# Multiplying 56 gating column tiles by the first two feature tiles ahead of their turn, with new chunk sizes

## The chip, the cores and the metric

One NeuronCore of a Trainium2 chip runs the whole program in one launch. The metric is device time in microseconds, the median of a few executions. One execution was also recorded by the hardware profiler, and every time below is from that record unless it is called a median. Engines are named as in the profile: PE multiplies matrices and PEld is its weight load, DVE and ACT are the vector and the scalar engine, POOL is GpSimd, SP issues all DMAs.

## The reference

One block of a diffusion backbone on 256 latent tokens and 256 context tokens, with 4096 features (16 tokens' rows and batch are dropped here):

```python
mod = jax.nn.silu(c) @ w_ada + b_ada                    # 4096 x 12288, c is a vector
shift, scale, gate = jnp.split(mod, 3, axis=-1)
h = modulate(rmsnorm(x, g_norm), shift[:, None], scale[:, None])
proj = h @ w_in                                         # 4096 x 16384
xa, xb, ga, gb = jnp.split(proj, [LRU_W, MIX_W, MIX_W + LRU_W], axis=-1)
hc = modulate(rmsnorm(ctx, g_norm), shift_c, scale_c)   # the same w_ada, on c_ctx
xa_c = hc @ w_in[:, :LRU_W]                             # context needs xa alone
ya, ya_c = rglru_branch(xa, xa_c, conv_w, conv_b, lam, w_r, b_r, w_i, b_i, ctx_out)
yb = pool_branch(xb.reshape(Bn, rows, GRID_W, POOL_W), w_pool, b_pool, pool_scale)
mixed = jnp.concatenate([ya * jax.nn.silu(ga), yb * jax.nn.silu(gb)], axis=-1)
x_new = x + gate[:, None] * (mixed @ w_out)             # 8192 x 4096
return rmsnorm(x_new, g_final)
```

All is float32. The kernel reaches that precision by splitting both sides of a product into a high part (`hi`, rounded to the fast float32r) and the rest (`lo`), and multiplying hi by hi, hi by lo and lo by hi.

## The kernel before

Activations lie with features on the 128 partitions and tokens along the free axis, so 4096 features are 32 feature tiles `x[k]` of 128 x 512: 256 latent tokens, then 256 context tokens. Weights come from HBM in tiles of 128 x 1024 (512 KB). `load_w` puts one into a buffer of the `raw` pool (6 buffers), lets ACT round it to `hi` (4 buffers, L97) and DVE or POOL subtract to get `lo` (3 buffers, L99). The vector products with `w_ada` take raw tiles as they are.

**Start.** All 32 x tiles are loaded and squared for the token statistics (L393 to L410). After every third one (`X_STEP`) a `w_ss` tile of the first chunk is loaded and multiplied on PE (L237). A product with ones (L412) gives the sums of squares, `rstd_of` the factor `rstd`, and `prep_h` makes of an x tile the modulated activation: times `rstd` on DVE (L300; L416 for the first chunk), scale and shift on ACT (L303), the split into `hhi` on ACT (L130) and `hlo` on DVE (L131).

**xa stage.** The features are handled in chunks (`CHUNKS`: two tiles, two, then four at a time, nine chunks in all; called c0 to c8 here). In chunk c PE multiplies the chunk's activations by all 32 column tiles of the xa part of `w_in`, three matmuls of 512 columns for each pair of feature and column tile (L337 to L339). The sums of the chunks are added in SBUF: c0 copies with ACT, later ones add with POOL (L345, L346) or DVE (L348). Under these matmuls the shift and scale columns of the next chunk are made: each `w_ss` tile is multiplied into an accumulator by DVE (L213, two instructions of 1024 columns for a tile) or, for `SHARES[c]` of a chunk's tiles, on PE (L237). At the chunk's end `rows` and `cols` turn the sums into columns (L237, L192, L202 to L204), three `prep_h` follow, and a fourth stands behind the chunk. A quarter of the chunk after the next is begun early (`EARLY`, `LAGS`).

**Gating stage.** PE multiplies the kept latent activations `hT` (32 tiles, hi beside lo) by the remaining 48 blocks of 256 columns of `w_in`: 16 pooling blocks, 16 gating blocks for yb, 16 gating blocks for ya. A block takes 8 weight tiles, each with 4 feature tiles x 2 halves x (one matmul of 512 columns, L566, and one of 256, L567). The evacuation of a gating block folds the two parts (L543, L548), applies the sigmoid and multiplies. The recurrent branch runs beside it, head by head, on DVE and ACT, with its own gate products (L478 to L480).

**Output stage.** 16 blocks of `w_out` by the mixed activations, the residual and the final norm, with the rest of the `gate` columns beside it.

The code writes a list of events; `run` issues the loads `LOOK` (4) weight tiles or `LOOK_A` (2) `w_ada` tiles ahead of their use. A scheduler then sets the order of each engine's instructions and of SP's DMAs, and engines run them in that order. The pools on which this change rests: `slots` (61 tiles of 128 x 512: x, `acc`, `hT` and more), `temps` (14), `ps_mm` (4 PSUM tiles of 512 columns).

## Time and profile before

| | us |
|---|---|
| median of 3 executions (2993.66 to 2999.54) | 2995.32 |
| span of the profiled execution | 2998.8 |
| start, up to the first xa matmul | 65.8 |
| xa stage | 803.9 |
| gating stage | 1354.3 |
| output stage with the end | 774.9 |

The profiled execution has no other time than its span on its page; the span lies 3.5 us above the median and within the three executions. The stages are cut at the first matmul of the next stage. In the rows further down a stretch's row gives its length, then for PE, PEld, DVE, ACT and POOL in this order how much of it the engine was busy (with the number of its instructions), the clock that PE was granted, the mean busy share of the 16 DMA engines, and the GB/s that they moved.

### The profile page before, as it was taken

How to read it: one execution, taken by the hardware profiler on the slowest of the kernel's cores; microseconds unless marked ns; L12 is line 12 of the kernel's file. 1: busy time of each engine (PE TensorE's matmuls, PEld its weight loads, DVE VectorE, ACT ScalarE, POOL GpSimd, SP SyncE). 2: the span in 40 equal slices, each digit the busy share in tenths (PEclk: the TensorE clock that was granted, in tenths of full speed). 3: DMA queues.
4: the chain of work that ended last, by engine and by line, in shares of the span. 5: the costliest groups of instructions: out<-in, count | busy, mean ns of one | idle time of the engine just before them, and what ended most of it. 6: DMA issues, size and time to landing. Idle time of an engine off the chain costs nothing.

```text
span 2998.8 us, 40342 instructions
## 1 busy us (share of the span) xinstructions
PE 2909.6 (97%) x14992; PEld 2405.3 (80%) x14992; DVE 2256.7 (75%) x2661; ACT 1559.9 (52%) x2112; POOL 530.7 (18%) x304
## 2 busy tenths in 40 slices
PE   5999999999999999999999999999999999999997
PEld 2656777778788888888888888888888888878886
DVE  6999999998447788888777777778888766665444
ACT  4442344434436666677666666666464443333442
POOL 1466777777520000000000000000000000000000
PEclk9999999999999999999999999999999999999998
DMA  8777787887365555565665566667978888786665
GB/s 301 279 261 252 262 263 261 272 277 250 126 183 176 176 177 175 179 183 172 186 185 181 185 188 189 196 195 251 326 232 318 318 288 286 264 279 216 193 191 171
DMA packets 201142, 679.47 MB, mean 227 GB/s; under 512 B 22000, under 2 KB 30320, under 8 KB 200944
## 3 DMA queue, kind: packets, MB, share of 16 engines
q1 hardware_dynamic: 200944, 676.89, 68.9%
q8 instruction: 117, 1.92, 0.3%
q14 instruction: 81, 0.66, 0.1%
HBM read 661.60 MB, written 15.20 MB: 226 GB/s over the span
## 4 chain that ended last, share of the span: by engine, by line
PE 84%; DVE 6%; DMA 6%; issue 1%; POOL 1%; ACT 1%; SPq 0%; DVEq 0%; POOLq 0%; ACTq 0%
PE mm L566 38%; PE mm L567 19%; PE mm L337 6%; PE mm L338 6%; PE mm L339 6%; DMA raw<-in_w_gate 4%; DVE wide L213 3%; PE wide L478 2%; PE wide L480 2%; PE wide L479 2%; PE mm L237 2%; DMA raw<-in_w_ss 1%; DMA x<-in_xc 1%; DVE lo L99 1%; DVE hlo L131 1%
## 5 line engine op out<-in xcount | busy, mean ns | idle before, releaser
L97 ACT CAST hi<-raw 128x1024 fp32r<-128x1024 f32 x832 | 871.9, 1049 | 968.6 <-PE mm L566 576.3
L99 DVE TENSOR_TENSOR lo<-raw,hi 128x1024 fp32r<-128x1024 f32 x704 | 856.5, 1221 | 371.5 <-PE mm L567 282.7
L566 PE MATMUL mm<-hT,hi 128*128 128x512 f32 x3072 | 1086.8, 399 | 0.0
L567 PE MATMUL mm<-hT,lo 128*128 128x256 f32 x3072 | 862.7, 281 | 0.0
L213 DVE SCALAR_TENSOR_TENSOR wide<-raw,sc,wide 128x1024 f32<-128x1024 f32 (+1 forms) x556 | 662.4, 1240 | 153.5 <-DMA raw<-in_w_gate 119.6
L566 PE MATMUL mm<-mix,hi 128*128 128x512 f32 x2048 | 724.7, 398 | 0.0
L566 PEld LDWEIGHTS mm<-hT,hi 128*128 128x128 f32 x3072 | 577.2, 188 | 144.5 <-ACT mix L130 0.9
L567 PE MATMUL mm<-mix,lo 128*128 128x256 f32 x2048 | 577.4, 282 | 15.3 <-DVE lo L99 15.1
L567 PEld LDWEIGHTS mm<-hT,lo 128*128 128x128 f32 x3072 | 580.2, 189 | 1.3
L566 PEld LDWEIGHTS mm<-mix,hi 128*128 128x128 f32 x2048 | 386.0, 188 | 95.1 <-ACT hi L97 1.7
L337 PE MATMUL mm<-hhi,hi 128*128 128x512 f32 x1024 | 404.1, 396 | 13.1 <-ACT hhi L130 10.7
L338 PE MATMUL mm<-hlo,hi 128*128 128x512 f32 x1024 | 402.1, 393 | 9.0 <-DVE hlo L131 9.0
L567 PEld LDWEIGHTS mm<-mix,lo 128*128 128x128 f32 x2048 | 388.2, 190 | 20.8 <-DVE lo L99 20.5
L339 PE MATMUL mm<-hhi,lo 128*128 128x512 f32 x1024 | 401.0, 392 | 0.0
L99 POOL TENSOR_TENSOR lo<-raw,hi 128x1024 fp32r<-128x1024 f32 x128 | 310.6, 2427 | 207.5 <-PE mm L339 87.8
L337 PEld LDWEIGHTS mm<-hhi,hi 128*128 128x128 f32 x1024 | 193.4, 189 | 73.0 <-ACT hhi L130 11.8
L346 POOL TENSOR_TENSOR acc<-acc,part 128x512 f32<-128x512 f32 x168 | 221.7, 1331 | 116.8 <-ACT part L345 115.8
L338 PEld LDWEIGHTS mm<-hlo,hi 128*128 128x128 f32 x1024 | 193.6, 189 | 53.3 <-DVE hlo L131 13.4
L339 PEld LDWEIGHTS mm<-hhi,lo 128*128 128x128 f32 x1024 | 193.6, 189 | 42.2 <-issue 1.7
L345 ACT COPY part<-mm 128x512 f32<-128x512 f32 x168 | 97.3, 584 | 155.4 <-PE mm L339 155.0
L348 DVE TENSOR_TENSOR acc<-mm,acc 128x512 f32<-128x512 f32 x88 | 60.1, 685 | 56.6 <-PE mm L339 56.5
L478 PE MATMUL wide<-uhi,hi 128*128 128x512 f32 x256 | 100.5, 393 | 0.0
(134 smaller groups left out, 2203.0 us busy)
## 6 DMA issues: line engine op xcount, KB each, us to landing
raw<-in_w_lat SPq DMA_DIRECT2D x384, 512.0 KB, 3.7
raw<-in_w_ss SPq DMA_DIRECT2D x256, 512.0 KB, 4.6
raw<-in_w_out SPq DMA_DIRECT2D x256, 512.0 KB, 4.6
raw<-in_w_xa SPq DMA_DIRECT2D x128, 512.0 KB, 4.4
raw<-in_w_gate SPq DMA_DIRECT2D x128, 512.0 KB, 4.8
raw<-in_w_rec SPq DMA_DIRECT2D x32, 512.0 KB, 3.6
raw<-in_w_pool SPq DMA_DIRECT2D x32, 512.0 KB, 3.7
x<-in_xc SPq DMA_DIRECT2D x32, 256.0 KB, 6.6
```

Of the source, the lines that this page charges most:

```text
L97: act.copy(out=hi, in_=raw)
L99: (eng or dve).tensor_tensor(out=lo, in0=raw, in1=hi.bitcast(F32), op=SUB)
L213: dve.scalar_tensor_tensor(out=accs[v][:, :width], in0=seg, scalar=s, in1=accs[v][:, :width], op0=MUL, op1=ADD)
L337: pe.matmul(out=ps, lhsT=wh, rhs=a, start=(k == 0), stop=False)
L338: pe.matmul(out=ps, lhsT=wh, rhs=b, start=False, stop=False)
L339: pe.matmul(out=ps, lhsT=wl, rhs=a, start=False, stop=(k == n - 1))
L345: act.copy(out=part, in_=ps)
L346: nc.gpsimd.tensor_tensor(out=acc[o], in0=acc[o], in1=part, op=ADD)
L348: dve.tensor_tensor(out=acc[o], in0=ps, in1=acc[o], op=ADD)
L478: pe.matmul(out=o, lhsT=wh[:, g, k, m], rhs=st["hi"][k], start=(k == 0), stop=False)
L566: pe.matmul(out=ps, lhsT=hi[:, k, m], rhs=a, start=first, stop=False)
L567: pe.matmul(out=ps[:, 0:T], lhsT=lo[:, k, m], rhs=a[:, 0:T], start=False, stop=last)
```

## The change

There are six edits that belong together.

1. **Ahead products.** `ahead_units` multiplies, during c0, the first two feature tiles' latent halves by the last 28 of the 48 blocks of the gating stage (blocks 20 to 47, which are 56 column tiles of gating columns): three matmuls of 256 columns for each feature tile and column tile. ACT copies the sums to 28 slots. The weights come as 14 tiles `w_lat0` of 512 KB.
2. **Spill and fetch.** `spill_ahead` writes 7 of these slots to HBM in each of c1 to c4. In the gating stage `fetch` loads a block's sums back into a temp after the block's fourth weight tile, and the evacuation adds them (one DVE instruction for each half). The first weight tile of these blocks is `w_lat2`, with two feature tiles in place of four (256 KB).
3. **Chunks** of 2, 4, 4, 4, 4, 4, 4, 4, 2 tiles in place of 2, 2, 4, 4, 4, 4, 4, 4, 4, still nine. The tiles on PE (`SHARES`) go from 16, 4, 11, 3, 0, 0, 0, 0, 0 to 16, 4, 2, 1, 1, 1, 1, 1, 0. In c0 an eighth, not a quarter, of the chunk after the next is begun early.
4. **x read twice.** Only the first six x tiles stay in SBUF; the others' slots are given to the ahead sums, and `load_x` reads the next chunk's tiles again at the start of c1 to c7. Their product with `rstd` is held in program order.
5. **Start.** One `w_ss` tile after every second x tile, not every third.
6. `softplus` of the recurrent branch's constants moves from behind c1 to ahead of c8. The slot pool has 68 tiles, not 61.

```diff
-X_STEP = 3
-SHARES = (16, 4, 11, 3, 0, 0, 0, 0, 0, 0, 0, 0)
-CHUNKS = (2, 2, 4, 4, 4, 4, 4, 4, 4)
+X_STEP = 2
+SHARES = (16, 4, 2, 1, 1, 1, 1, 1, 0)
+CHUNKS = (2, 4, 4, 4, 4, 4, 4, 4, 2)
+AHEAD = 28
+AHEAD_FROM = 48 - AHEAD
+SPILLS = 7
...
-                dve.tensor_tensor(out=x, in0=x, in1=rstd, op=MUL)
+                tc.keep_in_program_order(dve.tensor_tensor(out=x, in0=x, in1=rstd, op=MUL))
...
+            xt[k] = None
...
+    def load_x(k):
+        def f():
+            xt[k] = slot("x")
+            nc.sync.dma_start(out=xt[k], in_=xc[k])
+        return S_(f)
...
+    def ahead_units():
+        def unit(i):
+            def f(w):
+                hi, lo = (t.rearrange("p (b k m) -> p b k m", b=2, k=2) for t in w)
+                for b in range(2):
+                    blk = 2 * i + b
+                    ahead[blk] = slot("ahead")
+                    for j in range(2):
+                        ps = mm_tile()[:, 0:T]
+                        m = slice(j * P, (j + 1) * P)
+                        for k in range(2):
+                            hh, hl = (t[:, 0:T] for t in hc[k])
+                            pe.matmul(out=ps, lhsT=hi[:, b, k, m], rhs=hh, start=(k == 0), stop=False)
+                            pe.matmul(out=ps, lhsT=hi[:, b, k, m], rhs=hl, start=False, stop=False)
+                            pe.matmul(out=ps, lhsT=lo[:, b, k, m], rhs=hh, start=False, stop=(k == 1))
+                        act.copy(out=ahead[blk][:, j * T:(j + 1) * T], in_=ps)
+            return W_(w_lat0[i], f, nc.gpsimd)
+        return [unit(i) for i in range(AHEAD // 2)]
+
+    def spill_ahead(blk):
+        def f():
+            nc.sync.dma_start(out=ahead_sp[blk], in_=ahead[blk])
+            ahead[blk] = None
+        return S_(f)
...
-        xt.append(t)
+        xt.append(t if k < CHUNKS[0] + CHUNKS[1] else None)
...
+        if c == 0:
+            main = spread(main, ahead_units())
+        if c == NC - 1:
+            events.append(S_(softplus))
...
-            cut = len(nxt) // EARLY
+            cut = len(nxt) // (EARLY if c > 0 else 2 * EARLY)
...
+            if c > 0:
+                side = [spill_ahead(b) for b in range((c - 1) * SPILLS, min(AHEAD, c * SPILLS))]
+                main = spread(main, side, 0.0, 0.6)
+                events += [load_x(k) for k in range(k1, k1 + n1)]
...
-        if c == 1:
-            events.append(S_(softplus))
...
+        def fetch(blk):
+            def f():
+                early[blk] = temp("early")
+                nc.sync.dma_start(out=early[blk], in_=ahead_sp[base + blk - AHEAD_FROM])
+            return S_(f)
...
                 fold(ps, v[:, 0:T])
+                if blk in early:
+                    dve.tensor_tensor(out=v[:, 0:T], in0=v[:, 0:T], in1=early[blk][:, j * T:(j + 1) * T], op=ADD)
...
+            e = base + blk - AHEAD_FROM
+            if e < 0:
+                units += block_units([w_lat[base + blk, i] for i in range(8)], hT, evac(blk))
+            else:
+                srcs = [w_lat2[e]] + [w_lat[base + blk, i] for i in range(1, 8)]
+                u = block_units(srcs, hT, evac(blk), 2)
+                units += u[:4] + [fetch(blk)] + u[4:]
```

Three places show how the order moves. A name at the left of an arrow is what is written, those at its right what is read.

The first is DVE at the end of the start, where `rstd` is made and c0's two tiles are prepared. Before:

```order
L167 SCALAR_TENSOR_TENSOR rstd<-v,rstd 128x512
L416 TENSOR_TENSOR x<-x,rstd 128x512 x2
L300 TENSOR_TENSOR x<-x,rstd 128x512 x7
L202 TENSOR_TENSOR colB<-mm,vec 128x4
L203 TENSOR_TENSOR colA<-mm,vec 128x4
L300 TENSOR_TENSOR x<-x,rstd 128x512
L204 TENSOR_TENSOR colA<-colA,vec 128x4
L300 TENSOR_TENSOR x<-x,rstd 128x512 x4
L131 TENSOR_TENSOR hlo<-x,hhi 128x512
```

And now:

```order
L168 RECIPROCAL rstd<-s 128x512
L206 TENSOR_TENSOR colB<-mm,vec 128x4
L169 TENSOR_TENSOR v<-v,rstd 128x512
L207 TENSOR_TENSOR colA<-mm,vec 128x4
L170 TENSOR_TENSOR v<-v,rstd 128x512
L208 TENSOR_TENSOR colA<-colA,vec 128x4
L171 SCALAR_TENSOR_TENSOR rstd<-v,rstd 128x512
L455 TENSOR_TENSOR x<-x,rstd 128x512 x2
L215 TENSOR_SCALAR wide<-raw,sc_90 128x1024
L135 TENSOR_TENSOR hlo<-x,hhi 128x512
```

The products of later tiles with `rstd`, twelve of which stood around the columns, are gone from here, and the columns `colA` and `colB` stand ahead of `rstd`'s end.

The second is DVE at the border between two chunks of four tiles, from the last instruction on the next chunk's columns to its last `hlo`. Before, at the border of c2 and c3:

```order
L204 TENSOR_TENSOR colA<-colA,vec 128x8
L213 SCALAR_TENSOR_TENSOR wide<-raw,sc_90,wide 128x1024 x3
L348 TENSOR_TENSOR acc<-mm,acc 128x512
L131 TENSOR_TENSOR hlo<-x,hhi 128x512
L213 SCALAR_TENSOR_TENSOR wide<-raw,sc_90,wide 128x1024 x4
L131 TENSOR_TENSOR hlo<-x,hhi 128x512
L213 SCALAR_TENSOR_TENSOR wide<-raw,sc_90,wide 128x1024
L131 TENSOR_TENSOR hlo<-x,hhi 128x512
L213 SCALAR_TENSOR_TENSOR wide<-raw,sc_90,wide 128x1024
L348 TENSOR_TENSOR acc<-mm,acc 128x512
L131 TENSOR_TENSOR hlo<-x,hhi 128x512
```

And now, at the same border:

```order
L208 TENSOR_TENSOR colA<-colA,vec 128x8
L217 SCALAR_TENSOR_TENSOR wide<-raw,sc_90,wide 128x1024 x2
L304 TENSOR_TENSOR x<-x,rstd 128x512
L135 TENSOR_TENSOR hlo<-x,hhi 128x512
L217 SCALAR_TENSOR_TENSOR wide<-raw,sc_90,wide 128x1024
L359 TENSOR_TENSOR acc<-mm,acc 128x512
L304 TENSOR_TENSOR x<-x,rstd 128x512
L217 SCALAR_TENSOR_TENSOR wide<-raw,sc_90,wide 128x1024 x2
L135 TENSOR_TENSOR hlo<-x,hhi 128x512
L304 TENSOR_TENSOR x<-x,rstd 128x512
L217 SCALAR_TENSOR_TENSOR wide<-raw,sc_90,wide 128x1024 x3
L135 TENSOR_TENSOR hlo<-x,hhi 128x512 x2
```

Three products with `rstd` have come in (a fourth stands ahead of the columns); of the accumulators' instructions there are eight in place of nine, of the `acc` sums one in place of two.

The third is SP in c0. Before, its loads are `w_ss` tiles with an xa tile in between:

```order
L91 DMA raw<-in_w_ss 128x1024 x5
L91 DMA raw<-in_w_xa 128x1024
L91 DMA raw<-in_w_ss 128x1024 x4
L91 DMA raw<-in_w_xa 128x1024
L91 DMA raw<-in_w_ss 128x1024 x3
L91 DMA raw<-in_w_xa 128x1024
```

And now:

```order
L94 DMA raw<-in_w_ss 128x1024 x2
L94 DMA raw<-in_w_lat 128x1024
L94 DMA raw<-in_w_ss 128x1024 x2
L94 DMA raw<-in_w_lat 128x1024
L94 DMA raw<-in_w_ss 128x1024 x2
L94 DMA raw<-in_w_xa 128x1024
```

Between two xa tiles there are now one or two tiles of ahead weights (`w_lat0`, printed as `in_w_lat`), each behind two `w_ss` tiles, in the same pool of 6 buffers.

## Rows read from the trace of the kernel before

**Rows 1.** The page's first part: busy time of each engine, share of the span, instructions.

```profile
PE 2909.6 (97%) x14992; PEld 2405.3 (80%) x14992; DVE 2256.7 (75%) x2661; ACT 1559.9 (52%) x2112; POOL 530.7 (18%) x304
```

**Rows 2.** Stretches c0, c1, c2, c4, c7, c8, gating: length; engines' busy; PEclk; DMA share; GB/s.

```profile
65.77:126.86 61.09, 60.93 (x244) 40.39 (x244) 56.58 (x79) 31.08 (x49) 17.28 (x8) 0.96 0.74 256
126.86:200.20 73.34, 68.79 (x245) 40.47 (x245) 67.84 (x64) 24.05 (x38) 47.39 (x29) 0.98 0.77 269
200.20:309.77 109.57, 101.78 (x413) 74.29 (x412) 101.64 (x112) 45.19 (x76) 71.72 (x42) 0.97 0.71 247
...
406.24:500.00 93.76, 92.38 (x401) 73.41 (x400) 88.26 (x82) 39.20 (x62) 69.86 (x41) 1.00 0.80 269
...
687.47:781.25 93.78, 92.40 (x401) 73.36 (x400) 65.26 (x62) 35.06 (x52) 69.16 (x41) 1.00 0.69 228
781.25:869.64 88.39, 87.67 (x386) 71.92 (x384) 36.46 (x45) 26.84 (x40) 35.84 (x17) 1.00 0.45 136
869.64:2223.90 1354.26, 1354.24 (x7436) 1164.70 (x7435) 1050.71 (x1418) 900.33 (x1191) 0.00 (x0) 1.00 0.63 197
```

**Rows 3.** PE in time order (start, length, instruction), in c5 and c6.

```profile
599.96 0.39 PE L339 MATMUL mm<-hhi,lo 128*128 128x512 f32 x1
...
601.32 0.39 PE L339 MATMUL mm<-hhi,lo 128*128 128x512 f32 x1
...
660.80 3.60 PE L237 MATMUL mm<-fin,cst 128*4 128x512 f32 x8
...
670.01 1.05 PE L192 MATMUL mm<-cst,rows 4*128 4x4 f32 x8
```

**Rows 4.** One of PE's groups in the gating stage: count, busy us, mean ns.

```profile
L478 PE MATMUL wide<-uhi,hi 128*128 128x512 f32 x256 | 100.5, 393 | 0.0
```

**Rows 5.** PE and its weight loads in time order, in the gating stage.

```profile
1900.53 0.28 PE L567 MATMUL mm<-hT,lo 128*128 128x256 f32 x1
1900.64 0.40 PE L566 MATMUL mm<-hT,hi 128*128 128x512 f32 x1
...
1900.54 0.19 PEld L566 LDWEIGHTS mm<-hT,hi 128*128 128x128 f32 x1
```

**Rows 6.** The start: DMA rate (last column of rows 2), then DVE and ACT in time order.

```profile
6.00:40.00 34.00, 19.81 (x74) 6.27 (x75) 19.96 (x32) 19.00 (x31) 0.00 (x0) 1.00 1.03 391
...
42.63 1.13 PE L412 MATMUL mm<-ssq,ones 128*128 128x512 f32 x2 [1.03 <-DVE ssq L403]
...
50.81 3.46 DVE L416 TENSOR_TENSOR x<-x,rstd 128x512 f32<-128x512 f32 x2
54.19 8.59 DVE L300 TENSOR_TENSOR x<-x,rstd 128x512 f32<-128x512 f32 x7
...
63.62 1.58 ACT L303 ACTIVATE x<-x,colB,colA 128x256 f32<-128x256 f32 x3 [7.95 <-DVE colA L204]
```

**Rows 7.** DVE's instructions: accumulator mean in c4 to c6; min/median/max ns by line.

```profile
L213 DVE SCALAR_TENSOR_TENSOR wide<-raw,sc,wide 128x1024 f32<-128x1024 f32 x181 | 219.8, 1281 | 7.9 <-DMA raw<-in_w_ss 7.9
...
L300 DVE TENSOR_TENSOR x<-x,rstd x30: 675/682/2871, 54.2 to 374.3; 128x512 f32<-128x512 f32 x30
...
L131 DVE TENSOR_TENSOR hlo<-x,hhi x32: 675/753/2451, 65.9 to 787.6; 128x512 fp32r<-128x512 f32 x32
L300 DVE TENSOR_TENSOR x<-x,rstd 128x512 f32<-128x512 f32 x19 | 21.4, 1157 | 0.0
```

**Rows 8.** Work beside PE that the edits add more of: gating stage, then POOL.

```profile
L640 DVE TENSOR_TENSOR gv<-gv,gs 128x256 f32<-128x256 f32 x62 | 26.2, 423 | 13.5 <-ACT gs L638 12.6
L543 ACT COPY fold<-mm 128x256 f32<-128x256 f32 x127 | 46.1, 369 | 24.2 <-PE mm L567 24.1
L99 POOL TENSOR_TENSOR lo<-raw,hi x128: 2344/2411/2942, 51.1 to 853.7; 128x1024 fp32r<-128x1024 f32 x128
```

**Rows 9.** Busy time by stretch (columns of rows 2) around the two late stages' border.

```profile
2100.00:2200.00 100.00, 100.00 (x568) 86.75 (x567) 79.64 (x89) 46.89 (x60) 0.00 (x0) 1.00 0.89 306
2200.00:2400.00 200.00, 200.00 (x1122) 170.41 (x1121) 161.27 (x204) 103.26 (x162) 0.00 (x0) 1.00 0.84 295
```

## What the change does to the time: a prediction

> **What bounds the kernel now.** I read the page's busy times first, then the busy time stretch by stretch, then single instructions in order of time. PE is busy for 97% of the span [rows 1], but a busy PE needs a check stage by stage. In the gating stage PE is busy for 1354.24 of 1354.26 us [rows 2]: whatever is taken from PE there comes off the time. In the xa stage the chunks' rows tell two things. From c4 on, a chunk of four takes 93.76 us with PE busy 92.38 and DVE 88.26; c7 has only 65.26 us of DVE work and still takes 93.78, so PE sets the length there and DVE stands close behind. In c0 to c2 it is otherwise. An xa matmul of 512 columns comes every 0.227 us (six steps from 599.96 to 601.32 [rows 3]), so c0 and c1 need 192 x 0.227 = 43.6 us each for their matmuls and c2 needs 87.2; they take 61.09, 73.34 and 109.57, with DVE busy for 93% of each [rows 2]. These chunks wait for the next chunk's columns, and PE does part of that work itself in products that cost 0.45 us for a pass of 512 columns (3.60 us for eight [rows 3]) and half of it for one of 256.
>
> So the change has a place to gain: it puts matmuls out of the full gating stage into c0, where PE has room, and takes column products off PE. All terms below are against the profiled span, 2998.8 us, which lies 3.5 above the median; the difference is then applied to the median, 2995.3. About 6 us (0.2%) is what a measurement of this kernel can tell from no change.
>
> **Taken from the gating stage.** 28 blocks x 2 halves x 2 feature tiles = 112 pairs of matmuls. The stage's 7436 PE instructions [rows 2] are 768 matmuls of 512 columns for the recurrent gates (256 of L478 [rows 4], as many of L479 and L480), 12 small products of some 3 us, and 3328 pairs. A pair is worth (1354.26 - 768 x 0.227 - 3) / 3328 = 0.354 us, 112 of them **39.6 us**. What comes instead is hidden: 56 additions at 0.423 = 24 us on DVE [rows 8], less 28 halved weight subtractions, 28 x 0.6 = 17, on an engine with 1354 - 1051 = 303 us to spare [rows 2]. The bytes stay the same: 256 KB of sums come back where 256 KB of weights fall away. SP gets 28 loads that wait for a temp, and the weight loads queue behind them; the loads stand four tiles of some 2.8 us (8 pairs of 0.354) ahead of PE, which covers such a wait up to about that length. I take 0 for it.
>
> **Ahead products.** 28 x 2 x 2 x 3 = 336 matmuls of 256 columns in c0. They have as many columns as the 112 pairs of 768, so at the pair's pace, 0.354 / 3 = 0.118 each, they cost the same **39.6 us**. Such a matmul stands in the trace: the next one starts 0.11 us after it (1900.53 and 1900.64), and the next one's weight load starts with it, at 1900.54, not behind it [rows 5]. But here three such matmuls follow each other, which no row shows. The lower bound is half of a matmul of 512, 0.1135, or 38.1; the upper bound is a load's own 0.19, or 64. I take 0.118, from the same shape with the same load under it.
>
> The Trainium skill speaks against this price: "TensorE: Matmul & The Clock Gate", Part 3, The mechanism, has a weight load overlap with running matmuls only where the row group differs, and all of these use all rows. By that rule a matmul would cost its load and itself. The trace disagrees with it for pairs of 512 and 256 [rows 5]; the case that it is right for three 256s in a row is a rival below, priced from rows.
>
> Beside PE, c0 gets on ACT 14 roundings and 56 copies at 0.369, together 35 us, and on POOL 14 subtractions at 2.411, 34 us [rows 8]; with what they do in c0 now [rows 2], ACT then has 66 and POOL 51 us in a chunk of about 100. Both fit.
>
> **Start.** Fifteen, not ten, `w_ss` tiles now precede the last x tile: 5 x 0.524 MB at 391 GB/s = 6.7 us, so the product with ones moves from 42.63 to 49.3 [rows 6]. From there `rstd` takes 8.2 us as before (42.63 to 50.81). Gone are the seven products of later tiles, 8.59 us, between c0's own products and the columns; the columns are ready before `rstd` is. One product (half of 3.46) brings the time to 59.2, and ACT's 63.62 to PE's 65.77 before is 2.15 more: **61.3 in place of 65.8**. I give this 1.5 us either way.
>
> **The chunks.** PE's work and what it waits, with 1 us for `cols` [rows 3]. A steady chunk waits 93.76 - 87.2 - 3.6 - 1.0 = 2.0 us; c0, c1 and c2 wait 3.9, 8.9 and 12.4 by the same sum (40 short passes and 8 long, 44 long, 20 long).
> c0: 43.6 + 39.6 + 24 passes x 0.45 + 1.0 = 95.0, and a wait between 3.9 and 12.4, for which I take 7, near the mean of the old c0 and c1: 102.0.
> c1: 87.2 + 16 x 0.45 + 1.0 = 95.4 on PE. DVE has 34 unshared tiles where c4 has 32: 88.3 + 2 x 2 x 1.281 + 4 products with `rstd` at 1.157 [rows 7] = 98.0. At c4's ratio of busy to length (0.941) that is 104, with no gap at all 98: I take 101.
> c2 to c5: 87.2 + 12 x 0.45 + 1.0 = 93.6, and the border's 2.0. DVE loses one tile (2.6) and gains the four products (4.6), which gives 90.3 / 0.941 = 96.0; three of the four stand between the columns and the last `hlo`, worth some 1 us against the one accumulation and one sum that leave. So 96.6 each.
> c6 the same, 96.6; c7 has short passes, 87.2 + 1.8 + 0.6 + 2.5 = 92.1; c8 is half of the old one, 43.6 + 1.2 = 44.8. Softplus (the constants' small DVE work) moves out of c2, where DVE was full, to c8, where DVE was busy for 36 of 88 us; spilling and re-reading x add 28 and 26 transfers that nobody waits for soon.
> The xa stage thus ends at 61.3 + 102.0 + 101 + 4 x 96.6 + 96.6 + 92.1 + 44.8 = 884.2, against 869.6: 14.6 later. With 39.6 off the gating stage the sum is **-25.0 us**, 2970 by the median. The output stage is unchanged.
>
> **The rivals.**
> *The waits shrink to the steady ones.* c0 waits 3.9 and c1 to c6 2.0 us, DVE following: -3.1, -3.6, -5 and 1.5 at the start, 13 us better: 2957. For it: c7 shows that PE sets the pace. Against it: DVE is as full as PE.
> *DVE behind POOL.* A product with `rstd` takes 0.68 us at the median but up to 2.87, an `hlo` up to 2.45 [rows 7], where the 0.68 of work waits for POOL, whose weight subtraction takes 2.4 [rows 8]. If each of the four products waits a POOL instruction out, a chunk's DVE gains 4 x (2.4 - 1.2) = 4.8: 95.1 / 0.941 = 101, 4.5 more in each of c2 to c6 and about 5 in c0 and c1: +27, 2997, within 0.2% of no change. The Trainium skill, "SBUF — State Buffer", Who interferes with whom, has a DVE tensor_tensor of two SBUF inputs and a GpSimd instruction lock each other out for a whole instruction; the maxima agree. For it: POOL is busy for 70 of 94 us [rows 2]. Against it: in c0 and c1 the mean was 1.16.
> *Loads, the case on the slower side.* c0 now has 36 + 8 + 14 tiles, 30.4 MB; c1 30.1 MB with spills and x; c2 to c4 28.0 each; c5 26.2: 170.7 MB in the 589.4 us that I give them, 290 GB/s. The steady chunks ran at 269. If the six raw buffers let no more than that 269 through, these chunks take 634.6 us, 45.2 more: 3015. It decides against the change below 278 GB/s, where the extra is 25. For it: no chunk shown exceeds 269 [rows 2]. Against it: the DMA engines' share at 269 is 0.80, and 295 to 306 GB/s ran for 300 us with PE busy throughout [rows 9].
> *Weight loads not hidden.* A load (0.19) and a matmul (0.118) one after the other, 0.308 each: 336 x 0.19 = +64, 3033. It turns the sign from 0.118 + 25 / 336 = 0.192 a matmul on. Against it: the starts of the 256-column matmul and of the load beside it [rows 5].
>
> **How the numbers follow.** The forecast (2958 to 2981) gets 0.61, the shrunken waits 0.14, DVE behind POOL 0.12 (spread from 2982 to 3000), loads at 269 0.08, serial weight loads 0.05. Faster by over 0.2% (below 2989): 0.61 + 0.14 + half of 0.12 = 0.81. Within it: the other 0.06, and 0.03 of the loads' case at rates between, 0.09. Slower: 0.10. The range leaves out the slower cases with a part of the POOL case, and the best of the shrunken waits: 2951 to 2990.
>
> **What would show it.** Right: the gating stage about 39 us shorter with PE still without a gap; the first xa matmul near 61; 256-column matmuls 0.118 us apart; c0 near 102 and the steady chunks near 96.6. Wrong: PE waiting for `hlo` for over 4 us at each border (POOL), DVE waiting for `w_ss` tiles in c0 and c1 (loads), starts 0.19 us or more apart (weight loads), or any PE gap behind a fetch in the gating stage.

## The result: 1.6% slower, and where the time went

The changed kernel takes **3043.1 us** (median of 4 executions, 3039.9 to 3046.7) against 2996.2 before: a ratio of 1.0155, with a 95% interval of 1.0140 to 1.0169. The forecast was 2970, the range ended at 2990. The prediction was wrong in sign: +47 us in place of -25.

The profiled execution's span is 3038.2 us. Cut at the first matmul of the next stage, as before:

| us | before | forecast | after |
|---|---|---|---|
| first xa matmul | 65.8 | 61.3 | 64.0 |
| end of the xa stage | 869.6 | 884.2 | 941.7 |
| gating stage | 1354.4 | 1314.8 | 1327.7 |
| output stage, to its last `hi` matmul | 752.0 | 752.0 | 746.0 |

Against the forecast the xa stage ends 57.5 us late and the gating stage is 12.9 long; the output stage gives 6 back. That makes 64.4. The other 8.4 of the 73 us lie between profile and median: after's span is 4.9 below its median, the one before was 3.5 above the median that the forecast started from.

The profile after. First the page's busy times, then the chunks c0 to c8 and the gating stage in the columns of [rows 2]:

```profile
PE 2915.3 (96%) x15060; PEld 2416.7 (80%) x15060; DVE 2258.0 (74%) x2739; ACT 1577.2 (52%) x2182; POOL 559.8 (18%) x318
```

```profile
63.99:167.12 103.13, 100.68 (x560) 81.04 (x561) 85.04 (x77) 60.13 (x115) 50.30 (x21) 0.98 0.83 289
167.12:275.92 108.80, 99.83 (x410) 73.72 (x408) 95.24 (x89) 42.56 (x72) 64.86 (x37) 0.97 0.85 293
275.92:384.07 108.15, 98.68 (x404) 75.54 (x405) 92.57 (x88) 42.35 (x69) 71.99 (x42) 0.94 0.85 291
384.07:490.84 106.77, 98.30 (x406) 75.05 (x404) 90.70 (x85) 38.49 (x59) 70.22 (x41) 0.95 0.74 246
490.84:596.11 105.27, 97.19 (x405) 74.25 (x404) 88.30 (x84) 39.41 (x62) 70.16 (x41) 0.95 0.72 250
596.11:695.38 99.27, 96.00 (x405) 74.53 (x404) 85.56 (x80) 38.23 (x59) 69.55 (x41) 0.98 0.77 262
695.38:797.12 101.74, 97.52 (x406) 75.43 (x404) 82.86 (x92) 37.36 (x57) 69.24 (x41) 0.97 0.73 242
797.12:890.61 93.49, 90.87 (x397) 72.85 (x396) 36.95 (x56) 39.08 (x62) 70.10 (x41) 1.00 0.48 149
890.61:941.70 51.09, 46.32 (x193) 36.82 (x192) 43.00 (x72) 15.17 (x20) 15.35 (x9) 0.97 0.44 142
941.70:2269.42 1327.72, 1317.70 (x7213) 1133.21 (x7212) 1043.24 (x1476) 888.35 (x1202) 0.00 (x0) 1.00 0.65 201
```

c0 came as forecast (103.1; 102.0), c7 too. For c0 some of that is luck: its wait was put at a value between two bounds, and the same work takes from 102.8 to 108.5 us in other runs (e2, e7). c1 to c4 are 105 to 109 long instead of 97 to 101, with PE idle for 8 to 9.5 us in each and its clock at 0.94 to 0.97. Nothing like it stands in c4 before (93.76, idle 1.4, clock 1.00). The PE instructions in order of time show the idle time in c2 in one piece (a name in brackets is what ended it):

```profile
326.64 0.39 PE L349 MATMUL mm<-hlo,hi 128*128 128x512 f32 x1
326.86 0.39 PE L350 MATMUL mm<-hhi,lo 128*128 128x512 f32 x1
336.26 3.57 PE L241 MATMUL mm<-raw,sc 128*4 128x512 f32 x4 [9.01 <-DMA raw<-in_w_ss]
339.76 0.80 PE L348 MATMUL mm<-hhi,hi 128*128 128x512 f32 x1
340.36 0.63 PE L349 MATMUL mm<-hlo,hi 128*128 128x512 f32 x1
340.78 0.63 PE L350 MATMUL mm<-hhi,lo 128*128 128x512 f32 x1
...
342.33 0.40 PE L348 MATMUL mm<-hhi,hi 128*128 128x512 f32 x1
...
346.52 1.88 PE L241 MATMUL mm<-fin,cst 128*4 128x512 f32 x4
```

PE stands 9 us at the product of the one tile that `SHARES` leaves to it (called the shared tile below), with the chunk's other 168 xa matmuls queued behind. It then pays again: the same four products' worth takes 3.57 us where the `fin` products 6 us later take 1.88, and xa matmuls come 0.42 us apart for a while instead of 0.227. DVE meanwhile is still at the next chunk's columns, without a gap:

```profile
328.60 7.24 DVE L217 SCALAR_TENSOR_TENSOR wide<-raw,sc,wide 128x1024 f32<-128x1024 f32 x6
335.74 2.72 DVE L223 SCALAR_TENSOR_TENSOR fin<-raw,sc,wide 128x512 f32<-128x512 f32 x4
```

Such stops, 4.5, 9.2, 5.6 and 7.3 us more than the usual step, stand in c1 to c4, and none in c5 and c6. (c5 and c6 are 2.7 and 5.1 us over the forecast; PE's longest waits there are 3.9 us for `hhi` and 3.2 for `hlo`.)

What differs between c4 and c5? Counting the xa matmuls ahead of the columns' last products in PE's order tells it:

| | shared tile's product, after | `fin` products, after | of |
|---|---|---|---|
| before, c3 to c6 | none | 288 | 384 |
| after, c2, c3, c4 | 216 | 240 | 384 |
| after, c5 | 264 | 288 | 384 |

In c2 to c4 the products stand 48 matmuls, 48 x 0.227 = 11 us, earlier than before (in c1, with two shared tiles, some 20 matmuls), while DVE and the loads, which must be done first, are no earlier. Only c1 to c4 have spills in their lists. `spread` places the next chunk's column steps by counting entries of `main`; a spill is an entry that takes PE no time. About three quarters of the way through 16 weight tiles is tile 12 (288 matmuls). As far through 16 tiles and 7 spills is entry 17, of which 7 are spills: tile 10 (240).

That it is the entries and not the writes, the trace says already. The scheduler moved the 28 writes forward: one stands in c0, 10 in c1, 17 in c2, and the last starts at 371.8 us. c3 and c4 have no write and still their stop (the second line is c4's):

```profile
L390 SPq DMA_DIRECT2D ahead<-ahead x28: 422/425/961, 162.2 to 371.8; - x28
548.62 1.86 PE L241 MATMUL mm<-raw,sc 128*4 128x512 f32 x2 [7.13 <-DMA raw<-in_w_ss]
```

This theory came late. The first runs were made with others: the shared tile itself (theory A), the traffic of spills and second readings (theory B, the *Loads* rival), and the fixed place of the product with `rstd` (rival C).

### The profile page after: what moved, and what is told of

Its sections match the earlier page's. It is cut to its first block, busy times and chain, and to the rows that moved or that the text cites. A ratio compares the mean times of both kernels' runs of the same rounds, so it can differ in the third digit from the quotient of the medians.

```text
span 3038.2 us, 40825 instructions
## 1 busy us (share of the span) xinstructions
PE 2915.3 (96%) x15060; PEld 2416.7 (80%) x15060; DVE 2258.0 (74%) x2739; ACT 1577.2 (52%) x2182; POOL 559.8 (18%) x318
## 4 chain that ended last, share of the span: by engine, by line
PE 77%; DMA 9%; DVE 8%; issue 2%; ACT 2%; POOL 1%; SPq 0%; DVEq 0%; POOLq 0%; ACTq 0%
PE mm L614 35%; PE mm L615 18%; PE mm L348 5%; PE mm L349 5%; PE mm L350 5%; DMA raw<-in_w_gate 4%; DVE wide L217 3%; DMA raw<-in_w_ss 3%; PE wide L523 2%; PE wide L524 2%; PE wide L525 2%; PE mm L241 1%; DVE lo L103 1%; POOL lo L103 1%; DMA x<-in_xc 1%
## 5 line engine op out<-in xcount | busy, mean ns | idle before, releaser
L101 ACT CAST hi<-raw 128x1024 fp32r<-128x1024 f32 (+1 forms) x846 | 872.1, 1035 | 950.3 <-PE mm L614 530.1
L103 DVE TENSOR_TENSOR lo<-raw,hi 128x1024 fp32r<-128x1024 f32 (+1 forms) x704 | 840.9, 1201 | 367.7 <-PE mm L615 227.7
L614 PE MATMUL mm<-hT,hi 128*128 128x512 f32 x2960 | 1047.3, 399 | 0.0
L615 PE MATMUL mm<-hT,lo 128*128 128x256 f32 x2960 | 832.7, 281 | 0.8 <-DVE lo L103 0.8
L217 DVE SCALAR_TENSOR_TENSOR wide<-raw,sc,wide 128x1024 f32<-128x1024 f32 (+1 forms) x578 | 680.9, 1229 | 204.8 <-DMA raw<-in_w_gate 103.3
L614 PEld LDWEIGHTS mm<-hT,hi 128*128 128x128 f32 x2960 | 556.4, 188 | 137.8 <-ACT mix L134 0.9
L615 PEld LDWEIGHTS mm<-hT,lo 128*128 128x128 f32 x2960 | 560.0, 189 | 3.2 <-DVE lo L103 1.9
L103 POOL TENSOR_TENSOR lo<-raw,hi 128x1024 fp32r<-128x1024 f32 x142 | 344.4, 2426 | 209.6 <-PE mm L350 72.2
L241 PE MATMUL mm<-raw,sc 128*4 128x256 f32 (+1 forms) x172 | 59.9, 495 | 44.5 <-DMA raw<-in_w_ss 44.4
```

The source lines that it names most:

```text
L101: act.copy(out=hi, in_=raw)
L103: (eng or dve).tensor_tensor(out=lo, in0=raw, in1=hi.bitcast(F32), op=SUB)
L217: dve.scalar_tensor_tensor(out=accs[v][:, :width], in0=seg, scalar=s, in1=accs[v][:, :width], op0=MUL, op1=ADD)
L241: pe.matmul(out=st["rows"][0:4, :part], lhsT=lhsT, rhs=rhs, start=(st["n"] == 0), stop=(st["n"] == total - 1))
L614: pe.matmul(out=ps, lhsT=hi[:, k, m], rhs=a, start=first, stop=False)
L615: pe.matmul(out=ps[:, 0:T], lhsT=lo[:, k, m], rhs=a[:, 0:T], start=False, stop=last)
```

## The experiments

One table of all; "xa end" and "gating" as in the table above, from each run's own profile. The ratio is to the kernel before on the same chip; the kernel before has medians from 2992.1 to 2996.2 us on the chips used, so runs of different chips are better compared by their ratios. A profile is one execution and lies up to 8.6 us from its run's median (e9, 2986.0 for 2977.4); e16's is its slowest execution, 6.9 above. The runs e2, e5, e6, e9 and e15 leave the ahead sums out of the output.

| run | median us | ratio (95%) | xa end | gating |
|---|---|---|---|---|
| e1_no_share | 3024.6 | 1.0101 (1.0086-1.0116) | 923.1 | 1327.1 |
| e2_no_spill | 3020.5 | 1.0091 (1.0069-1.0113) | 933.9 | 1314.9 |
| e3_before_share | 3018.2 | 1.0080 (1.0065-1.0095) | 894.4 | 1354.4 |
| e4_no_order | 3033.5 | 1.0130 (1.0102-1.0158) | 927.8 | 1327.6 |
| e5_no_reread | 2979.0 | 0.9937 (0.9917-0.9956) | 889.6 | 1315.4 |
| e6_ring9 | 2970.8 | 0.9913 (0.9888-0.9939) | 891.0 | 1314.6 |
| e7_three | 3003.2 | 1.0026 (1.0014-1.0039) | 921.4 | 1316.1 |
| e8_six_ahead | 3002.5 | 1.0023 (1.0012-1.0034) | 880.6 | 1350.0 |
| e9_ring6 | 2977.4 | 0.9941 (0.9926-0.9956) | 894.5 | 1316.4 |
| e10_twenty | 2985.7 | 0.9975 (0.9963-0.9986) | 893.4 | 1325.9 |
| e11_before_ring9 | 2979.1 | 0.9951 (0.9936-0.9966) | 859.2 | 1354.5 |
| e12_twenty_free | 2964.1 | 0.9900 (0.9885-0.9915) | 871.9 | 1326.0 |
| e13_share_ring9 | 2993.9 | 0.9989 (0.9979-0.9998) | 872.5 | 1354.5 |
| e14_spill_kept | 3026.7 | 1.0102 (1.0087-1.0117) | 929.0 | 1326.9 |
| e15_three_undone | 2968.9 | 0.9911 (0.9894-0.9927) | 884.2 | 1313.4 |
| e16_spill_in_step | 3017.2 | 1.0072 (1.0044-1.0100) | 921.9 | 1329.5 |
| e17_whole28 | 2986.4 | 0.9963 (0.9951-0.9975) | 898.8 | 1315.2 |
| e18_whole20 | 2961.6 | 0.9891 (0.9868-0.9913) | 870.6 | 1326.0 |

### One suspect at a time

```diff
-SHARES = (16, 4, 2, 1, 1, 1, 1, 1, 0)
+SHARES = (16, 4, 0, 0, 0, 0, 0, 0, 0)
```

> The changed kernel with no column tile of chunks 2 to 8 left to TensorE (in the changed kernel two, then one a chunk, the last of each chunk, stand in TensorE's order as products straight from the raw load). Theory A (TensorE stops in its order at that last tile, 4.5 to 9.2 us a chunk, 44 us in all, and its clock falls to 0.94 to 0.95 behind the stop): the chunks 1 to 5, 99 to 109 us long in the changed kernel, fall to 96 to 99, and the whole to 2995 to 3010 us. Theory B (the spills and the second reading of x on the same queue hold up the other loads): the chunks stay within 2 us of what they were and the whole at 3038 to 3048; if VectorE, which gets one tile (2.5 us) more a chunk, is what paces them, it rises to 3050 to 3056.

3024.6: the tile on PE costs 18.6 us, by the median and by the end of the xa stage, not the 44 that theory A named. c3 to c5 fell to 99, but c1 grew to 113.8, and a new stop stands there (waits of PE in c1; us in all, times, longest):

```profile
PE mm L241 <- DVE fin L223: 16.1, 1, 16.1
```

With the shared tile gone PE waits at nearly the same place, after 240 of 384 matmuls, for the other products. That should have told me to look at the place.

```diff
-            nc.sync.dma_start(out=ahead_sp[blk], in_=ahead[blk])
...
-                units += u[:4] + [fetch(blk)] + u[4:]
+                units += u
```

> The changed kernel without the 28 spill writes, and without the 28 fetches and their additions in the gating stage (these partial sums are left out of the output). Theory B: the chunks 1 and 2, which hold the 28 spills, fall from 108 to 109 us to 97 to 100, 20 us in all; chunks 3 to 6 stay. Theory A: the chunks stay within 2 us each. The gating stage: if the fetched tiles and their additions cause its 13 us over forecast (stops of TensorE at the pool products and gate products), it falls from 1327.7 to about 1315; if the thinner first weight tiles or the scheduler's order do, it stays at 1326 to 1330. Whole: 3010 (B and fetch), 3030 (fetch alone), 3040 (neither).

The end of the xa stage moved by 7.8 us only, and the stops stayed (the row below is c2's). The spills' entries are still in the list here. The gating stage fell by 12.8, to what the forecast had (1314.9; 1314.8).

```profile
332.61 1.87 PE L241 MATMUL mm<-raw,sc 128*4 128x512 f32 x2 [9.80 <-DMA raw<-in_w_ss]
```

In the kernel before:

```diff
-SHARES = (16, 4, 11, 3, 0, 0, 0, 0, 0, 0, 0, 0)
+SHARES = (16, 4, 11, 3, 1, 1, 1, 1, 1)
```

> The kernel before with one column tile of each of its chunks 4 to 8 moved from VectorE to TensorE (five tiles, ten matmuls of 0.45 us). Theory A: the chunks 3 to 7, in which these products stand, grow from 93.8 to 98 to 104 us each by a stop at that tile, 20 to 45 us in all, 3018 to 3040. Theory B: only the products' own 0.9 us a chunk, 2996 to 3002.

3018.2, +22.8 us, though the products stand at 264 and 288 here: a shared tile costs by itself. PE hardly waits at it; what grows is DVE's wait for its loads, over four chunks from some 20 to 51 us.

```profile
DVE wide L213 <- DMA raw<-in_w_ss: 50.7, 36, 5.0
```

```diff
-                tc.keep_in_program_order(dve.tensor_tensor(out=x, in0=x, in1=rstd, op=MUL))
+                dve.tensor_tensor(out=x, in0=x, in1=rstd, op=MUL)
```

> The changed kernel without the instruction that keeps the multiplication of x by its reciprocal in program order on VectorE (three characters' worth of the change; the scheduler may place it freely again, as in the kernel before). Theories A and B: nothing, 3035 to 3050. Rival C (that fixed place makes VectorE late, and the 9 us stop at the last column tile of a chunk is its result): the chunks 1 to 5 fall by 5 us or more each, 3010 to 3020.

3033.5 in two executions. Its interval overlaps that of the changed kernel; the xa stage ends 13.9 us earlier. A part of rival C, to be seen clearly further down.

### Traffic, the ring of raw buffers, and the fetches

All five runs here have no shared tile in c1 to c7. e5, e6 and e9 also have no spills and no fetches, this time with their entries gone:

```diff
-            if c > 0:
-                side = [spill_ahead(b) for b in range((c - 1) * SPILLS, min(AHEAD, c * SPILLS))]
-                main = spread(main, side, 0.0, 0.6)
```

> The changed kernel with no tiles left to TensorE in chunks 2 to 8, no spills, no fetches, and x kept in its slots from the first reading on (each partial sum of the first chunk is computed and then dropped, so 28 of the gating sums lack their first two feature tiles in the output). Beside the run with no tiles shared, it takes away 28 spills, 28 fetches and 26 readings of x, all of 256 KB. Loads theory (the queue passes about 269 GB/s in a steady chunk, whatever it carries): chunk 1 falls from 113.8 to 98 to 101, chunk 2 from 103.8 to 94 to 98, chunks 3 to 5 from 98.9 to 94, the end of the xa stage from 923 to about 884, the whole to 2960 to 2970 us. Rival C (the fixed place of the multiplication on VectorE): chunks 3 to 5 stay at 98 to 99, the whole 2975 to 2985.

> The changed kernel with no tiles shared, no spills and no fetches (partial sums dropped as in the run before), but x read twice as in the changed kernel, and nine raw buffers instead of six (slots 61 instead of 68). If the six raw buffers set the 269 GB/s (a load waits until the sixth load before it is used up): chunks 3 to 5 fall from 98.9 to 94 to 95 although every byte is still moved, c0 too from 104 to 97 to 100. If the DMA engines themselves set it: chunks 3 to 5 stay at 98 to 99 and chunk 0 at 104. Whole: 2960 to 2972 by the first, 2980 to 2995 by the second.

Both end the xa stage near 890 and fell below the kernel before; e5's whole lies in the range of rival C, e6's in that of the raw buffers. But e5 keeps x and has six raw buffers, e6 reads x twice and has nine: they differ in two things. e9, x read twice with six buffers, stands between them.

> The run with nine raw buffers again, but with six (and 68 slots): no tiles shared, no spills and fetches (partial sums dropped), x read twice. It parts the second reading from the spills. Ring theory (six raw buffers pass about 269 GB/s, and each 256 KB more on the queue costs 0.97 us of a chunk): chunk 1 (6 readings of x more than without) 105 to 107 against 100.4, chunks 2 to 5 98 to 99 against 94 to 97, the xa stage's end 900 to 908 against 889.6, and 891 with nine buffers; whole 2984 to 2992. Rival (the second reading is free and the spills alone cost the 33 us between the runs with no tiles shared): end of the stage 890 to 893, whole 2970 to 2976.

The rival won, though the run lies 1.4 us past its range: c1 to c6 are within 1 us of those of e5, and the stage ends 4.9 us later, 3.2 of it in c0, where nothing is read again. The ratios of the whole, 0.9941 and 0.9937, are the same within their intervals. **The second reading of x costs next to nothing**, and six buffers are no ceiling of 269 GB/s (c1 of e9 runs at 289). What e1 has and this run has not, spills with their entries, is worth 28.6 us of the xa stage.

```diff
+    def with_fetch(unit, fetch):
+        def f(w):
+            fetch[1]()
+            unit[2](w)
+        return ("w", unit[1], f, unit[3])
...
-                units += u[:4] + [fetch(blk)] + u[4:]
+                u[4] = with_fetch(u[4], fetch(blk))
+                units += u
```

> The changed kernel, with its whole computation, with three things taken back: no tiles shared in chunks 2 to 8, the multiplication of x free in its place, and the fetch of a partial sum made inside the fifth weight tile's step, so that it is no entry of its own among the steps over which the recurrent pieces are spread. By the runs so far: the first is worth 18.5 us (3024.6 against 3043.1), the second about 10 (3033.5). Third: if the entries only slid the recurrent pieces against the pool products (the stops of 4.9 and 2.3 us stand ahead of the first fetch), the gating stage falls from 1327.5 to 1317 to 1320; if the addition and its buffers are the cost, it stays at 1326 to 1329. Whole: 3005 or 3015.

3003.2, the lower of the two values. The gating stage is 1316.1, within 2 us of that without any fetch (1314.9): the fetch and the addition are all but free, and their 28 entries cost 12 us, by the same fault. `spread` lays the recurrent pieces over the list by count, so 28 more entries late in it push every piece; PE stops at two pool products, at 1098.6 and 1356.3 us, ahead of the first fetch at 1599.3. After, and then e7, PE's waits in the gating stage:

```profile
PE mm L614 <- DVE yb L593: 6.9, 2, 4.7
PE wide L523 <- ACT i L537: 1.2, 1, 1.2
```

```profile
PE wide L523 <- ACT i L537: 1.1, 1, 1.1
```

> The changed kernel with 6 instead of 28 gating blocks begun in the first chunk, their sums kept in slots until the gating stage (no spill, no fetch), x kept from the first reading on, and no tiles shared in chunks 2 to 8. The whole computation. Loads theory: chunk 0 falls from 104 to 85 to 92 (11 weight tiles fewer on the queue), chunks 1 and 2 as in the run without second reading (99, 96), chunks 3 to 5 94; end of the xa stage 866 to 874; the gating stage 1354.4 less 6 x 4 x 0.354 = 1346; whole 2978 to 2990. Rival C: 4 to 5 us more for each of the chunks 2 to 6, 2998 to 3010.

c0 did fall (83.8), and c1 took it back: 108.9, with a stop of 12.2 us for `fin`. c0 and c1 are 192.7 together, as with 20 blocks ahead in e12 (193.7) and e18 (193.4). DVE is busy for 178.7 of the 192.7, so its work for the columns of c1 and c2 probably sets that sum, and fewer ahead products win nothing there; but e12 and e18 have nine buffers and the free place, and no run shows it alone. The gating stage gained 4.4 us where 8.5 were expected of 6 blocks; why is open.

### Nine raw buffers

```diff
-RAWB, HIB, LOB = 6, 4, 3
+RAWB, HIB, LOB = 9, 4, 3
...
-    spool = ctx.enter_context(tc.tile_pool(name="slots", bufs=68))
+    spool = ctx.enter_context(tc.tile_pool(name="slots", bufs=61))
...
-AHEAD = 28
+AHEAD = 20
```

> The changed kernel, whole, with what the runs point to: no tiles shared in chunks 2 to 8, nine raw buffers and 61 slots, 20 gating blocks ahead instead of 28 (as many as 61 slots hold), five spills a chunk, the fetch inside the fifth weight tile's step. Ring theory: chunk 0 92 to 98, chunk 1 96 to 102 with its spills, chunks 2 to 5 96, end of the xa stage 884 to 892; gating stage 1354.4 less 28.3 and 1 more = 1327; output 745; whole 2975 to 2988, faster than the kernel before. If the spills cost on the queue as they did with six buffers: chunks 1 and 2 105 each, 2990 to 3000.

> The kernel before with nine raw buffers instead of six and nothing else (the room comes from the smaller buffer for DMA descriptors, as in the change). Ring theory: its steady chunks (93.75 us, TensorE 92.4 us busy) have no wait for loads to lose, so they gain under 1 us each; chunks 0 and 1 (61.1 and 73.3 us, with 6.6 us of waits of TensorE for the raw loads there) and 2 (109.6) may lose up to 25 us together: 2970 to 2996. If the buffers matter only for what the change adds: 2992 to 2998.

> The run with 20 blocks ahead and nine buffers, with the multiplication of x by its reciprocal free in its place on VectorE. With six buffers and spills the free place was worth 10 us (3043 to 3033). Rival C (the fixed place by itself makes VectorE late): again 8 to 12 us. If it only mattered where VectorE waited for loads anyway: within 3 us of the run with 20 blocks.

e10 is 0.25% faster than before, with c1 at 108.0, near the 105 given for spills that cost on the queue. e11 shows that the buffers give the old kernel 13 us (2979.1 for 2992.1 on the same chip; c1 67.3 for 73.3, c2 102.9 for 109.6). Their room comes from a smaller buffer for DMA descriptors, which the changed kernel has too and the old one has not; it was not run by itself. So with equal buffers e10 is still 6.5 us slower than the old kernel. Freeing the product with `rstd` gives e12, by that one edit on the same chip, 21.6 us: **rival C is right**, and the stage shows how. The instructions on the x tiles around the border of c5 and c6, e10 and then e12 (count, ns min/median/max, first and last start):

```profile
L304 DVE TENSOR_TENSOR x<-x,rstd x4: 678/679/714, 637.3 to 652.2; 128x512 f32<-128x512 f32 x4
L135 DVE TENSOR_TENSOR hlo<-x,hhi x4: 680/1574/2441, 642.2 to 656.7; 128x512 fp32r<-128x512 f32 x4
```

```profile
L304 DVE TENSOR_TENSOR x<-x,rstd x6: 677/1776/2282, 597.7 to 606.3; 128x512 f32<-128x512 f32 x6
L135 DVE TENSOR_TENSOR hlo<-x,hhi x4: 755/1430/2446, 628.2 to 640.7; 128x512 fp32r<-128x512 f32 x4
```

Kept in program order, the four products stand one by one at the border (c6 begins at 652.2), and each tile's chain of DVE, ACT, ACT, DVE starts only there; the last `hlo` comes 4.5 us after the border. Left free, the products stand 32 to 41 us ahead of the border, which is at 638.2 in e12 (the row counts six, with two that go by their order to c7). They are longer there (1.78 us at the median), and the chunk is still 4.5 us shorter (c5, 93.2 for 97.7).

> The kernel before with nine raw buffers, and with one tile of each of its chunks 4 to 8 moved to TensorE. With six buffers the move cost 22.8 us (3018.2 against 2995.3), 5.0 to 6.7 us in each chunk that held the products. If a shared tile costs because its raw buffer stays occupied until TensorE comes to it (a sixth of the ring gone, VectorE then waits for its own loads): nine buffers bring the cost from 22.8 to 5 to 10 us, the products' own 0.9 us a chunk and TensorE's change of operand among it, 2984 to 2990. If the stop is TensorE's own order alone: 20 to 25 us again, 2999 to 3005.

By the ratios 11 us above e11 (14.7 by the medians, which are of two chips), between the two answers. In c5 to c7 the cost falls to 2.0, 2.1 and 1.7 us (it was 6.7, 5.9 and 3.2), and DVE's wait for its loads, over c4 to c7, all but goes. So the ring of raw buffers carries most of the cost in these chunks: a raw buffer that waits for PE's turn is one that DVE's loads lack. c3 still loses 6.6; why is open.

```profile
DVE wide L213 <- DMA raw<-in_w_ss: 4.7, 8, 1.1
```

### The place of the products

```diff
-            nc.sync.dma_start(out=ahead_sp[blk], in_=ahead[blk])
+            tc.keep_in_program_order(nc.sync.dma_start(out=ahead_sp[blk], in_=ahead[blk]))
```

> The changed kernel with no tiles shared in chunks 2 to 8, as in the run at 3024.6, and each spill kept at the place in SP's order where the program writes it: seven a chunk in the chunks 1 to 4. In the trace of that run the scheduler had put 23 of the 28 spills into chunk 1 (113.8 us) and 5 into chunk 2 (103.8). If the spills cost by the queue's time, wherever they stand: chunk 1 falls to 104 to 107, chunks 2 to 4 stand at 100 to 102, the end of the stage moves by less than 6 us, 3018 to 3026. If the bunch is what costs (chunk 1 is late for its loads anyway, the later chunks have room): the end moves from 923 to 900 to 910, 3000 to 3012.

> The changed kernel with no tiles shared in chunks 2 to 8, no spills and fetches (partial sums dropped), and the multiplication of x free in its place: all three suspects undone at once, with x read twice, 28 blocks ahead and six raw buffers kept. The forecast ended the xa stage at 884.2 us; the changed kernel ended it at 941.7, and the run with the first two undone at 894.5. If these three are the whole of the miss there: 876 to 886, whole 2958 to 2968. If the second reading of x or the shape of the chunks has a part of its own: it stays at 890 to 895, whole 2974 to 2978.

e14: c1 stays at 113.8 with seven writes as with 23. Neither number nor bunching of the writes makes c1 long. e15 ends the stage at 884.2 us, the very number of the forecast: shared tile, spills and fixed place make up the miss there. That the two agree to the tenth is luck: e15's start is 3.4 us late, c0 5.0 and c8 4.6 longer than forecast, c1 4.8 and c2 to c6 together 7.9 shorter, and the forecast had the shared passes in it. Which side of the spills, e16 tells:

```diff
+    def with_after(unit, steps):
+        def f(w):
+            unit[2](w)
+            for s in steps:
+                s[1]()
+        return ("w", unit[1], f, unit[3])
...
-                main = spread(main, side, 0.0, 0.6)
+                main = [with_after(m, [s for j, s in enumerate(side) if int(0.6 * len(main) * j / len(side)) == i])
+                        for i, m in enumerate(main)]
```

> The changed kernel, whole, with one thing moved: each spill is made at the end of a w_xa weight tile's step, and is no entry of its own in the list over which the column tiles of the next chunk are spread. Same spills, same queue, same chunk (tiles shared, fixed place and fetches kept). In the changed kernel the last products of the columns stand in TensorE's order after 240 of a chunk's 384 xa matmuls in chunks 2 to 4 (the shared tile's after 216), and after 288 (264) in chunk 5, which has no spills, and in the run without entries; here they stand after 288 (264) in the chunks 1 to 5. Entry theory (seven entries that take no time of TensorE slide the columns' products 48 matmuls, 11 us, ahead of VectorE): the stops of 4.7 to 9.4 us ahead of the shared tile's products go, chunks 1 to 4 fall from 105 to 109 to 99 to 102, the end of the xa stage from 941.7 to 912 to 922, whole 3012 to 3024. Spills as traffic (queue, slots): no change, 3038 to 3047.

3017.2: **25.9 us by the medians, 25 by the ratios, with the same work, the same spills and the same queue**. The products stand after 264 and 288 in c2 to c4 (277 and 288 in c1); in the xa stage PE's wait at the shared tile falls, after first and then e16, from 27.2 us to 5.2 (4.5 of it in c1):

```profile
PE mm L241 <- DMA raw<-in_w_ss: 27.2, 5, 9.0
```

```profile
PE mm L241 <- DMA raw<-in_w_ss: 5.2, 2, 4.5
```

> The changed kernel, whole, with 28 blocks ahead, six raw buffers and x read twice, and the three causes taken away: no entries for spills and fetches (both made inside a weight tile's step), no tiles shared in chunks 2 to 8, the multiplication of x free in its place. Entry theory: the xa stage ends as in the run without spills (884.2), up to 5 us more for the spills' own traffic; gating stage 1316, output 746; whole 2968 to 2978, the amount of the forecast. Spills as traffic: the stage ends at 900 to 915, whole 2985 to 3000.

2986.4, above the 2968 to 2978 of the entry theory and in the range given for spills as traffic, but 0.37% faster than before, with all of the change's computation. The gating stage is as forecast (1315.2). The xa stage ends 14.6 us after e15's, over c1 to c4; in c1 the queue carries 320 GB/s, well above 269, and c3 (100.0) and c4 (98.5) are long though no write is left there:

```profile
172.03:272.13 100.10, 95.81 (x400) 74.50 (x401) 95.29 (x90) 40.39 (x70) 66.97 (x39) 0.97 0.91 320
272.13:368.33 96.20, 94.00 (x401) 74.39 (x400) 91.29 (x83) 39.01 (x62) 69.67 (x40) 0.98 0.88 302
368.33:468.31 99.98, 95.00 (x401) 74.83 (x400) 93.30 (x88) 39.55 (x61) 69.83 (x40) 0.97 0.76 265
```

So the spills cost something beyond their entries. Whether it is traffic, the slots that they keep, or the order that the scheduler makes of it stays open.

> The run with 20 blocks ahead, nine raw buffers and the free place (2964.1), with the spills made inside a weight tile's step too. There the last products stood after 264 and 240 of 384 in the chunks 1 and 2 to 4, with stops of 9.3 and 3.1 us in chunks 1 and 2; here after 288. Entry theory: chunk 1 falls from 103.5 to 94 to 97, chunk 2 from 96.9 to 94, whole 2952 to 2960. Spills as traffic: 2962 to 2966.

2961.6: against the 2964.1 of e12 no more than the executions scatter (0.9891 and 0.9900), and between the two answers. c2 fell as expected (93.7), c3 rose (96.1 for 93.2), c1 hardly moved (102.1): there PE still stops for 5.8 us for DVE's `fin`, with the products after 288, so DVE's columns and not the place come last. With 20 blocks, nine buffers, no shared tile and the free `rstd` product, the products' early place costs next to nothing: the stage ends 1.3 us sooner without the entries, where it was 19.8 in the changed kernel. It is the fastest version, 1.1% below the kernel before where e11 is 0.5% below it, so the change is worth 0.6% beside the buffers.

## Why the prediction was wrong, point by point

**The chunks** is the step that failed. It put 2.0 us of waits to each steady chunk because c4 before has them, and took the order of PE's instructions for unchanged. Spills it put at nothing, as transfers "that nobody waits for soon". The order of the changed kernel lay open, and I read DVE's border and SP's loads there, but not where PE's L241 stood. The 57.5 us divide, along the runs from the changed kernel to e15, into: 19.8 for the spills' entries (e16), 23.1 for the shared tile and the fixed place (e17), 14.6 for the rest of the spills (e15), by what is still open. Of the 23.1 the fixed place has about 10 (e9 against e15, 894.5 and 884.2, both without spills). A shared tile was priced as two passes on PE and a relief for DVE; it is a wait in PE's order and a buffer out of the ring. The three products near the border were priced at 1 us a chunk, some 5 in all; fixed in their place they cost 10 (e9 against e15) to 21 (e10 against e12).

**Taken from the gating stage** was right: without fetches the stage is 1354.4 - 39.5 (e2), for 39.6. The zero for the fetch was right for the load and the addition (39.2 and 38.4 less in e17 and e7, which have both) and wrong for its entry in the list, 12 us.

**Ahead products** were right, 0.120 us apart (first and 48th of a run in c0: 5.63 / 47) for 0.118, and their weight loads, 0.19 us each on all 128 rows, start 0.12 us apart too:

```profile
80.27 0.28 PE L381 MATMUL mm<-hhi,hi 128*128 128x256 f32 x1
...
85.90 0.28 PE L383 MATMUL mm<-hhi,lo 128*128 128x256 f32 x1
...
80.87 0.19 PEld L381 LDWEIGHTS mm<-hhi,hi 128*128 128x128 f32 x1
80.99 0.19 PEld L382 LDWEIGHTS mm<-hlo,hi 128*128 128x128 f32 x1
```

That settles *weight loads not hidden*: three 256s in a row hide their loads as [rows 5] has it, and the Trainium skill's rule on row groups ("TensorE: Matmul & The Clock Gate", Part 3, The mechanism) does not hold here. (The rival's time, 2970 + 64, comes to 3034 and not 3033.)

**Start**: 64.0 for 61.3. The product with ones came as forecast (48.8 for 49.3), but from there to the first product with `rstd` it took 12.3 us, not 8.2: two of its 0.69 us steps on DVE now fall beside POOL's first three subtractions, which before began as `rstd` ended (51.10; [rows 6] has 50.81 for what follows `rstd`). DVE and POOL in order of time:

```profile
54.82 2.79 DVE L169 TENSOR_TENSOR v<-v,rstd 128x512 f32<-128x512 f32 x1
57.65 2.71 DVE L170 TENSOR_TENSOR v<-v,rstd 128x512 f32<-128x512 f32 x1
60.39 0.69 DVE L171 SCALAR_TENSOR_TENSOR rstd<-v,rstd 128x512 f32<-128x512 f32 x1
...
52.41 7.40 POOL L103 TENSOR_TENSOR lo<-raw,hi 128x1024 fp32r<-128x1024 f32 x3 [51.28 <-ACT hi L101]
```

**c8** was 6.3 us over. PE waits 2.6 us there for DVE's `acc` sums and 2.2 for `hhi`; no run takes either away.

**The rivals.** *Loads* gave 634.6 us for c0 to c5, and 631.4 were measured: close, for another reason. Six buffers pass 320 GB/s (e17), the second reading is free (e9), and c3 and c4 are 10.2 and 8.7 us over the forecast at 246 and 250 GB/s, below the 269. *DVE behind POOL* cost 4 us at the start, but not in the chunks: there it needed 2.4 us for each product with `rstd`, and in the changed kernel they take 0.69 at the median, with no wait of PE for `hlo` over 3.2:

```profile
L304 DVE TENSOR_TENSOR x<-x,rstd x30: 677/686/2887, 157.9 to 891.4; 128x512 f32<-128x512 f32 x30
```

In e12 they are held up more and the chunks are shorter. None of the rivals was an order that the list makes by itself. A chance of 0.10 for slower was too small for a change that moves work through such a list.

## What to carry to other kernels

Where a helper spreads steps by counting list entries, an entry that costs no time moves everything else: attach stores and fetches to the step that they belong to, and compare the place of each engine's waiting instruction, in work ahead of it, before and after. When undoing the suspects one at a time finds less than the miss, ask what every run still has in common: shared tile, spill writes and fixed place gave 18.6, 7.8 and 13.9 us of the xa stage alone, and all these runs kept the entries. With the entries' 19.8 they add up to 60.1, near the 57.5 of all together, so the suspects hardly hid one another. An in-order instruction on raw data ties up a ring buffer until its engine's turn comes, and a forced place is worth a look at what stood there when the scheduler chose.

## What was not expected of the hardware

A stop of PE costs more than its length: behind the 9.0 us in c2, four products took 3.57 us instead of 1.88, and the six xa steps from 339.76 to 342.33 took 2.57 instead of 6 x 0.227 = 1.36, so 2.9 us on top; PE's granted clock in these 6 us is 0.52, near the lower of its two levels (1.2 of 2.4 GHz), and 1.00 right behind them:

```profile
336.26:342.33 6.07, 6.07 (x10) 2.39 (x11) 6.07 (x8) 0.00 (x0) 0.00 (x0) 0.52 1.00 350
342.33:347.00 4.67, 4.67 (x21) 3.33 (x20) 1.27 (x2) 1.18 (x2) 1.56 (x2) 1.00 0.96 346
```

The mean over the chunk is 0.94, where c4 to c8 of the kernel before, with PE idle for at most 1.4 us in each, have 1.00. Six buffers of 512 KB carried 320 GB/s over 100 us with PE busy for 96 of them (e17, c1), with the DMA engines at a share of 0.91.
